# Padding three small SBUF tables so that the big ones start at multiples of 64 bytes

## The chip, the cores and the metric

The kernel runs on one core of a Trainium2 chip. The time is the device time of one execution in microseconds (us), as a median of three runs; lower is better. A profile of one execution on the chip goes with it. All work is in float32, and there is one launch.

## The reference

The input is 256 tokens of 1024 features. A first block computes a root-mean-square norm, one wide projection (queries, keys, values, a recurrent input and three gates), banded attention with 16 heads, a causal convolution with a gated linear recurrence, the two output projections, a merge, a residual, and a gated feed-forward layer. A second block runs four more gated feed-forward layers, a chunked spatial gating unit between the first two of them, and stick-breaking attention between the last two:

```python
def swiglu(h, w_in, w_out):
    gu = h @ w_in
    gate, up = jnp.split(gu, 2, axis=-1)
    return (jax.nn.silu(gate) * up) @ w_out
...
x = x + FFN_RES_SCALE * swiglu(rms_norm(x, ffn_norm[i, 0]), ffn_w_in[i, 0], ffn_w_out[i, 0])
h = rms_norm(x, mix_norm[i])
...
return rms_norm(x, final_norm)
```

Nearly all arithmetic is products of 256 tokens with weight matrices that are read once each.

## The kernel before

**Weights.** The host lays all weights out as 240 groups of 1 MB, 128 partitions by 2048 elements, in the order in which they are used (`PLAN`). SyncE's queue loads a group into one of three buffers `raw` (`load`). A group is two chunks of 128 by 1024. `prep` turns a chunk into two float32r tiles: ScalarE copies `raw` into `h` (line 162), which rounds it, and VectorE writes the remainder `raw - h` into `l` (line 163). There are eight buffers each of `h` and `l`, and `refill` prepares chunks up to seven ahead of their use.

**Activations.** They are split in the same way into a high and a low part: `xh` and `xl` (8 feature tiles of 128 by 256 each), and the four tables `rr0` to `rr3` of that size.

**Products.** A product of two split operands is three TensorE matmuls into the same PSUM bank (`mm3`): high by high, high by low, low by high. All matmuls are issued at line 210. In most of them the stationary operand is 128 columns of `h` or `l`, and the moving one is 256 columns of `xh`, `xl` or an `rr`: a chunk is 24 of these. In the value projection, the spatial gate's first half and the last layer's output (`pe_nat`, `pe_rn`) it is the other way round: 128 columns of the activations are stationary and 512 columns of `h` or `l` move. A few others are plain float32, of which the trace records two matmuls for each one that is issued, and 56 are bfloat16.

**Order.** Everything is issued in one fixed order written by hand. While TensorE works on a chunk, small generators (`rounds`) issue a step of other work each: scaling by the norm's factor, the gates' functions, attention, the recurrence.

**Placement.** `sb(name, shape)` takes a table out of one pool. The tables lie in the order in which they are asked for, each rounded up to 32 bytes per partition, behind a start at a multiple of 64 bytes (byte 16512). `par` is 200 floats, 800 bytes, which is 32 past a multiple of 64. So `x0` to `x3`, `xh`, `xl`, `rr0` to `rr3` and `sa` all start 32 bytes past a multiple of 64. `sa` is 2072 floats, 8288 bytes, again 32 past one, so the next tables (`sb`, `sc`, `sd`, `sf`, `sg`, `sh`, `ident`, `ones`) start at multiples of 64. Behind some small tables follow `ntri`, `nones`, `identb`, `maskb` (at multiples), more small tables, and then `raw`, `h` and `l`, all 32 bytes past one. Slices inside the big tables step by multiples of 64 bytes.

Of the kernel before, what the change touches and what calls it, by code (L numbers as in the profile page):

```python
# [100 lines left out]
NPAR = 0  # L101
# [5 lines left out]
class Builder:  # L107
# [67 lines left out]
        self.gens.append(gen)  # L175

    def refill(self, most=2):
        """prepares the weights to come, more of them once the first loads have landed"""
        ahead = LA if self.ci > 12 else 4
        for _ in range(most):  # L180
            if self.preps < self.ci + ahead:
                self.prep()
# [97 lines left out]
        self.nc.gpsimd.tensor_tensor(dst, src, self.mhalf[:, 0:src.shape[1]], op=ALU.pow)  # L280

    def bcast_mm(self, bank, half, col, start):
        """a factor per token (partition) to a row on every partition"""
        for t in range(2):
            self.mm(bank[:, half, t * 128:(t + 1) * 128], col[:, t:t + 1].to_broadcast([128, 128]), self.ident,
                    start and t == 0, True)

    def stats_a(self, pool=None, kv=False):
        """squares to the per-token factor column"""
        nc = self.nc  # L290
        self.st = (pool or self.acc)()
        self.R, self.rcol = (self.Rkv, self.rckv) if kv else (self.Rt, self.rc)
        self.stat_mm(self.sq[0], self.st, 0, True)
        nc.vector.tensor_scalar(self.v2, self.st[:, 0, 0:2], 1.0 / D, 1e-6, op0=ALU.mult, op1=ALU.add)
        self.rpow(self.rcol, self.v2)

    def stats_b(self):
        """the factors on every partition"""
        self.bcast_mm(self.st, 1, self.rcol, False)
        self.nc.scalar.activation(self.R, self.st[:, 1, :], AF.Copy)  # L300

# [15 lines left out]

    def setup(self):
        nc, dram = self.nc, self.dram
        self.P = self.sb("par", [128, NPAR])  # L320
        self.X = [self.sb(f"x{p}", [128, 2, 256]) for p in range(4)]
        self.XS = (self.sb("xh", [128, 8, 256], F32R), self.sb("xl", [128, 8, 256], F32R))
        self.RR = [self.sb(f"rr{i}", [128, 8, 256], F32R) for i in range(4)]
        self.SA = self.sb("sa", [128, 8 * 259])
        self.SL = {c: self.sb("s" + c, [128, 2048]) for c in "bcdfgh"}
        self.ident = self.sb("ident", [128, 128])
        self.ones = self.sb("ones", [128, 128])
        self.mhalf = self.sb("mhalf", [128, 2])
        self.Rt = self.sb("rt", [128, 256])
        self.R1 = self.sb("r1t", [128, 256])  # L330
        self.Rkv = self.sb("rkv", [128, 256])
        self.rckv = self.sb("rckv", [128, 2])
        self.v2 = self.sb("v2", [128, 2])
        self.rc = self.sb("rc", [128, 2])
        self.tiny = self.sb("tiny", [128, 1])
        self.c8 = self.sb("c8", [128, 8])
        self.nc8 = self.sb("nc8", [128, 8])
        self.half = self.sb("half", [128, 24])
        self.sq = self.view("b", 4)
        nc.scalar.dma_start(self.P, dram["par"])  # L340
        x_load = lambda p: nc.sync.dma_start(self.X[p], dram["x"][:, 2 * p:2 * p + 2, :])
        for f in range(2):
            nc.sync.dma_start(self.X[0][:, f, :], dram["x"][:, f, :])  # L343
        self.warm_up()
        for g in range(2):
            t = self.rawp.tile([128, 2048], F32, tag="raw", name="raw")
            for c in range(2):
                if 2 * g + c:
                    x_load(2 * g + c)
                n = 512 if 2 * g + c == 0 else 1024  # L350
                for o in range(c * 1024, (c + 1) * 1024, n):
                    nc.sync.dma_start(t[:, o:o + n], dram["w"][g, :, o:o + n])  # L352
            self.raw[g] = t
        self.loads = 2
        self.load()
        self.gw = self.SL["h"].rearrange("p (a b) -> p a b", b=128)
        make_identity(nc, self.ident)
        nc.gpsimd.memset(self.ones, 1.0)
        nc.gpsimd.memset(self.mhalf, -0.5)
        nc.gpsimd.memset(self.tiny, 2.0 ** -115)  # L360

    def warm_up(self):
        """keeps the tensor engine busy while the first operands are on their way"""
        nc = self.nc
        nc.vector.memset(self.SL["c"][:, 0:64], 0.0)
        junk = self.SL["c"][:, 0:64].bitcast(BF16)
        bank = self.wk()
        for _ in range(40):
            self.mm(bank[:, 0, 0:128], junk, junk, True, True)
        nc.scalar.preload_act_table_set("exp_and_others")  # L370
# [7 lines left out]
        for gi in range(2):  # L378
            self.group(kinds, lambda c, h, l, s: self.pe_k(h, l, s[2], self.XS, outs), fills=fills[gi])

    # ---------------------------------------------------------------- block 1
    def block1(self):
        nc, dram = self.nc, self.dram
        SA, SL, RR = self.SA, self.SL, self.RR
# [7 lines left out]
        xr = SA.rearrange("p (a b) -> p a b", b=259)  # L392
# [4 lines left out]
        it = SL["d"].rearrange("p (a b) -> p a b", b=256)  # L397
# [1 line left out]
        gb = SL["g"].rearrange("p (a b) -> p a b", b=256)  # L399
        ga = SL["h"].rearrange("p (a b) -> p a b", b=256)  # L400

        # xr
        w = ("A", "w_in")
        b = [self.wk(), self.wk()]
        self.start_k((("K", "w_in"),) * 2, [b[0][:, 0, :], b[0][:, 1, :], b[1][:, 0, :], b[1][:, 1, :]])
# [31 lines left out]
        for p in range(4):  # L437
            a_group(mul_ev(ga, p))

        # v, tokens on partitions  # L440
        V = SL["c"].rearrange("p (t c) -> p t c", c=1024)
        for cg in range(2):
            banks = [self.wk(), self.wk()]
# [7 lines left out]
            for gi in range(2):  # L451
                self.group((("K", "w_in"),) * 2,
                           lambda c, h, l, s: self.pe_nat(h, l, s[2], self.XS, banks),
                           end=(lambda: self.spawn(v_ev())) if gi else None)

        # attention state
        qk = self.carve("b", 0, 2, 512)
        PT = self.carve("b", 1024, 2, 384) + self.carve("d", 1536, 1, 384) + self.carve("f", 1536, 1, 384)
        bias = self.carve("d", 0, 2, 768)
# [82 lines left out]

        qk_group(0)

        # rnn_out
        accs = [self.acc() for _ in range(4)]
        for r in range(4):
            self.group((("R", "rnn_out"),) * 2,
# [10 lines left out]
        for j in range(1, 8):  # L559
            qk_group(j)  # L560

        # attn_out, merged with the recurrent branch
        accs2 = [self.acc() for _ in range(4)]
        MH, ML = RR[0], RR[1]
        for r in range(3):
# [13 lines left out]
        self.tail_group("attn_out", (6, 7), lambda k: (OH[:, k, :], OL[:, k, :]), accs2, merge, merge_l)  # L579
        self.drain()  # L580

        # w_o and the residual
        gf = lambda k: ("norm_ffn_g", k)
        for half in range(2):
            b = [self.wk(), self.wk()]
# [10 lines left out]
            for gi in range(2):  # L596
                self.group((("K", "w_o"),) * 2,
                           lambda c, h, l, s: self.pe_k(h, l, s[2], (MH, ML), outs),
                           end=fin if gi else None)
# [106 lines left out]
                    yield  # L706

    def tail_group(self, name, ks, zf, accs, fin, fin_l):
        """last two rows of weights, output by output, each pair finished as it comes"""
        g = self.gi  # L710
        assert [c[:3] for c in PLAN[g]] == [("R", name, k) for k in ks], (PLAN[g], name, ks)
        hl = [self.take()[:2] for c in range(2)]
        self.rounds(1)
        for p in range(4):
            for o in (2 * p, 2 * p + 1):
                for i, k in enumerate(ks):
                    s = slice(o * 128, o * 128 + 128)
                    zh, zl = zf(k)
                    self.mm3(accs[p][:, o % 2, :], hl[i][0][:, s], hl[i][1][:, s], zh, zl, start=False, stop=(i == 1))
            fin(p)  # L720
            if p:
                fin_l(p - 1)
        fin_l(3)
        self.rounds(1)
        self.refill()

    # ---------------------------------------------------------------- feed-forward
    def ffn(self, n, fin, fin_l, stats=None, nat=False, more=None):
        nc = self.nc
        a, r = ("A", f"{n}_in"), ("R", f"{n}_out")  # L730
# [56 lines left out]
        return accs  # L787

    def pe_rn(self, h, l, zh, zl, accs, first, last, banks=range(4)):
        """a row block of weights as the moving operand: tokens on partitions"""  # L790
        for b in banks:
            t, cg = divmod(b, 2)
            out = accs[b].rearrange("p a b -> p (a b)")
            s, ts = slice(cg * 512, cg * 512 + 512), slice(t * 128, t * 128 + 128)
            self.mm(out, zh[:, ts], h[:, s], first, False)
            self.mm(out, zh[:, ts], l[:, s], False, False)
            self.mm(out, zl[:, ts], h[:, s], False, last)
# [19 lines left out]
            self.split_l(p, self.X, g, xs)  # L817
        return fin, fin_l

    # ---------------------------------------------------------------- block 2  # L820
    def block2(self):
        nc, dram, P = self.nc, self.dram, self.par
        SA, SL, RR = self.SA, self.SL, self.RR

        # end of block 1: x2 = h * r1 * g1, next input x2 * r2 * g2
        XG = self.view("c", 4)

        def fin(p, bank):
# [71 lines left out]
        self.ffn("f3", fin, fin_l, stats=(lambda: self.stats_a(kv=True), sb3))  # L900
        self.squares(self.X, self.sq)

        # keys and values from the state before that feed-forward layer
        Kt = SL["c"][:, 0:512].rearrange("p (a b) -> p a b", b=256)
        Vt = SL["c"][:, 512:1024].rearrange("p (t c) -> p t c", c=256)
        kb, vb = self.acc(), self.acc()
# [33 lines left out]
        assert not self.gens  # L940

    def final_bank(self, b, bank):
        """the last norm and the output"""
        nc = self.nc
        t, cg = divmod(b, 2)
        flat = bank.rearrange("p a b -> p (a b)")
# [1 line left out]
        s0, s1, v, r = self.ss[:, t, 0:1], self.ss[:, t, 1:2], self.v2[:, t:t + 1], self.rc[:, t:t + 1]  # L948
# [15 lines left out]
    def sgu(self, fin, fin_l):  # L964
# [29 lines left out]
                if c % 2:  # L994
                    yield

        # gate half, tokens on partitions
        def v_ev(banks, cg):
            sl = slice(cg * 512, (cg + 1) * 512)
            for t in range(2):  # L1000
# [33 lines left out]
        a = ("A", "a_in")  # L1034
# [8 lines left out]
        UH, UL = (RR[0], RR[1]), (RR[2], RR[3])  # L1043

        def mix(p):
            """token mixing of feature tiles 2p, 2p+1 and the product with u"""
            bank = self.wk()
            for f in range(2):
                c = 2 * p + f
# [203 lines left out]


def stick_order():
    """heads in the order of the tiles: two heads of neighbouring key/value heads each"""
    cols = []
    for T in range(8):
        kp, t = divmod(T, 4)
        for h in (2 * kp * 4 + t, (2 * kp + 1) * 4 + t):  # L1260
            cols.extend(range(h * 64, h * 64 + 64))
    return np.array(cols)
# [82 lines left out]
```

## Time and profile before

| | |
|---|---|
| median of 3 runs | 1462.52 us (1462.49 to 1462.91) |
| span of the profiled execution, first to last instruction | 1460.8 us |
| outside the span (median less span) | 1.7 us |
| TensorE, matmuls | 1451.3 us busy, 99% |
| TensorE, weight loads | 1413.2 us busy, 97% |
| VectorE | 950.9 us busy, 65% |
| ScalarE | 734.7 us busy, 50% |
| weights moved | 257 MB read, 177 GB/s over the span |

The time of an execution is its span and what lies around it; the profiled one is 1.7 us short of the median. Matmuls are pipelined: the profile gives each a duration from its start to its modelled end, and they overlap. What a matmul costs in a stream is therefore not its duration but the distance from its start to the next one's start, called the pitch below.

### The profile page before, as it was taken

What the parts mean: (1) busy time and instruction counts of PE and PEld (TensorE: products, weight loads), DVE (VectorE), ACT (ScalarE), POOL (GpSimd) and SP (SyncE); (2) the same over time, 40 slices, a digit from 0 to 9 for tenths busy, and PEclk for the clock granted to TensorE, in tenths of its full rate; (3) what the DMA queues carried; (4) which work ended last, traced back from release to release, by engine and by line L of the source; (5) the groups of instructions that cost most, each with busy time, mean ns of one, the idle gap of its engine ahead of it and who ended that gap; (6) DMA issues with size and microseconds to landing.
All of it is one profiled execution on the core that took longest, in us unless ns stands there. A gap on an engine that the chain in (4) does not pass through costs nothing.

```text
span 1460.8 us, 26958 instructions
## 1 busy us (share of the span) xinstructions
PE 1451.3 (99%) x11548; PEld 1413.2 (97%) x11548; DVE 950.9 (65%) x1316; ACT 734.7 (50%) x1094; POOL 24.8 (2%) x57
## 2 busy tenths in 40 slices
PE   9999999999999999999999999999999999999998
PEld 9998999999999999998999999999999998999997
DVE  6976677665557765576775655567655576655563
ACT  5677465544445544455445444445444467544442
POOL 0000000000000000000000000000000000000000
PEclk9999999999999999999999999999999999999999
DMA  8555444454454555546444555544555542445451
GB/s 293 199 186 198 177 163 174 173 202 174 176 188 155 194 185 189 195 178 221 170 155 164 189 186 177 191 181 164 190 196 195 179 174 87 159 145 196 180 182 49
DMA packets 37624, 260.31 MB, mean 178 GB/s; under 512 B 4224, under 2 KB 4608, under 8 KB 7040
## 3 DMA queue, kind: packets, MB, share of 16 engines
q1 hardware_dynamic: 36288, 253.77, 48.7%
q0 software_dynamic: 1072, 4.72, 1.0%
q8 instruction: 90, 1.47, 0.4%
q14 instruction: 30, 0.25, 0.0%
q10 hardware_dynamic: 144, 0.10, 0.0%
HBM read 257.53 MB, written 1.05 MB: 177 GB/s over the span
## 4 chain that ended last, share of the span: by engine, by line
PE 99%; DMA 0%; ACT 0%; DVE 0%; SPq 0%; issue 0%; POOLq 0%; POOL 0%
PE wk L210 62%; PE acc L210 36%; DMA raw<-w 0%; PE acc L521 0%; PE wk L521 0%; ACT sf L959 0%; ACT sd L949 0%; DVE l L163 0%; ACT h L162 0%; SPq L352 0%; SPq L343 0%; DVE sf L950 0%; POOLq L1341 0%; POOL rc L280 0%; ACT sh L1134 0%
## 5 line engine op out<-in xcount | busy, mean ns | idle before, releaser
L163 DVE TENSOR_TENSOR l<-raw,h 128x1024 fp32r<-128x1024 f32 (+1 forms) x479 | 570.8, 1219 | 241.0 <-ACT h L162 240.4
L210 PE MATMUL wk<-xh,h 128*128 128x256 f32 x2272 | 646.8, 285 | 1.2 <-ACT h L162 1.2
L210 PE MATMUL wk<-xh,l 128*128 128x256 f32 x2272 | 643.9, 283 | 0.1
L210 PE MATMUL wk<-xl,h 128*128 128x256 f32 x2272 | 643.6, 283 | 0.0
L162 ACT ACTIVATE h<-raw 128x1024 fp32r<-128x1024 f32 (+1 forms) x479 | 485.7, 1044 | 64.6 <-PE acc L210 30.1
L210 PEld LDWEIGHTS wk<-xh,h 128*128 128x128 f32 x2272 | 436.7, 192 | 4.0 <-ACT h L162 1.8
L210 PEld LDWEIGHTS wk<-xl,h 128*128 128x128 f32 x2272 | 436.7, 192 | 0.5
L210 PEld LDWEIGHTS wk<-xh,l 128*128 128x128 f32 x2272 | 436.5, 192 | 0.6 <-DVE l L163 0.6
L210 PE MATMUL acc<-rr,h 128*128 128x256 f32 x2016 | 367.2, 284 | 0.0
L210 PEld LDWEIGHTS acc<-rr,h 128*128 128x128 f32 x2016 | 314.3, 192 | 1.9 <-issue 1.9
L210 PE MATMUL acc<-rr,l 128*128 128x256 f32 x1008 | 285.2, 283 | 0.0
L210 PEld LDWEIGHTS acc<-rr,l 128*128 128x128 f32 x1008 | 193.4, 192 | 0.0
L738 ACT ACTIVATE sa<-sa 128x256 f32<-128x256 f32 x110 | 45.4, 417 | 285.6 <-DVE sa L306 285.4
L309 ACT ACTIVATE rr<-sa 128x256 fp32r<-128x256 f32 (+1 forms) x122 | 52.7, 439 | 185.8 <-DVE sa L743 128.9
L306 DVE TENSOR_TENSOR sa<-wk,rt 128x512 f32<-128x512 f32 x92 | 62.3, 686 | 91.0 <-PE wk L210 73.1
L310 DVE TENSOR_TENSOR rr<-sa,rr 128x256 fp32r<-128x256 f32 (+1 forms) x122 | 54.2, 451 | 53.3 <-ACT rr L309 53.3
L210 PE MATMUL acc<-h,rr 128*128 128x512 f32 (+1 forms) x208 | 63.1, 374 | 0.0
L210 PEld LDWEIGHTS acc<-h,rr 128*128 128x128 f32 x208 | 38.7, 189 | 6.7
L258 ACT ACTIVATE xh<-x,par 128x256 fp32r<-128x256 f32 x56 | 25.2, 501 | 33.8 <-DVE x L316 18.6
L210 PE MATMUL acc<-l,rr 128*128 128x512 f32 (+1 forms) x104 | 38.9, 374 | 0.0
L743 DVE TENSOR_TENSOR sa<-sa 128x256 f32<-128x256 f32 x88 | 37.0, 428 | 0.0
L210 PE MATMUL wk<-rr,h 128*128 128x256 f32 x192 | 34.8, 283 | 0.0
(253 smaller groups left out, 970.2 us busy)
## 6 DMA issues: line engine op xcount, KB each, us to landing
raw<-w SPq DMA_DIRECT2D x237, 1024.0 KB, 4.9
sd<-bias POOLq DMA_DIRECT2D x8, 384.0 KB, 3.3
raw<-w SPq DMA_DIRECT2D x3, 512.0 KB, 8.3
sh<-gates SPq DMA_DIRECT2D x1, 1024.0 KB, 9.1
out<-sf SPq DMA_DIRECT2D x4, 256.0 KB, 2.1
x<-x SPq DMA_DIRECT2D x3, 256.0 KB, 7.4
raw<-w SPq DMA_DIRECT2D x2, 256.0 KB, 4.4
sa<-ws POOLq DMA_DIRECT2D x1, 512.0 KB, 3.7
```

The source lines that it names most:

```text
L162: nc.scalar.activation(h[:, s], raw[:, s], AF.Copy)
L163: nc.vector.tensor_tensor(l[:, s], raw[:, s], h[:, s].bitcast(F32), op=ALU.subtract)
L210: self.nc.tensor.matmul(out, lhsT, rhs, start=start, stop=stop, skip_group_check=True)
L258: self.nc.scalar.activation(xs[0][:, k, :], src[p][:, f, :], AF.Copy, scale=self.par(*g(k)))
L306: self.nc.vector.tensor_tensor(dst, bank, self.Rpair(), op=ALU.mult)
L309: self.nc.scalar.activation(zh, src, AF.Copy)
L310: self.nc.vector.tensor_tensor(zl, src, zh.bitcast(F32), op=ALU.subtract)
L738: nc.scalar.activation(t[:, 0, :], t[:, 0, :], AF.Silu)
L743: nc.vector.tensor_tensor(t[:, 1, :], t[:, 0, :], t[:, 1, :], op=ALU.mult)
```

## The change

Three tables are asked for with more columns than are used, and then cut to the columns used. `par` grows from 800 to 896 bytes, `sa` from 8288 to 8320, and `rckv` (8 bytes, 32 with rounding) to 64. No instruction is added, removed or moved; the order and all shapes are the same. Some comments go too.

```diff
-        self.P = self.sb("par", [128, NPAR])
+        self.P = self.sb("par", [128, 224])[:, 0:NPAR]
...
-        self.SA = self.sb("sa", [128, 8 * 259])
+        self.SA = self.sb("sa", [128, 2080])[:, 0:8 * 259]
...
-        self.rckv = self.sb("rckv", [128, 2])
+        self.rckv = self.sb("rckv", [128, 16])[:, 0:2]
```

By the sizes, `x0` to `x3`, `xh`, `xl`, `rr0` to `rr3` and `sa` move up by 96 bytes, to multiples of 64. The tables behind `sa` move by 128 and keep their place within 64 bytes: `sb` to `sh`, `ident` and `ones` at multiples, `rt`, `r1t` and `rkv` 32 past one. All behind `rckv` moves by 160: `raw`, `h` and `l` come to lie at multiples of 64, and `ntri`, `nones`, `identb` and `maskb` 32 past one.

## Rows read from the trace of the kernel before

**Rows 1.** The page's head and part 1: busy time, share of the span, instructions.

```profile
span 1460.8 us, 26958 instructions
...
PE 1451.3 (99%) x11548; PEld 1413.2 (97%) x11548; DVE 950.9 (65%) x1316; ACT 734.7 (50%) x1094; POOL 24.8 (2%) x57
```

**Rows 2.** The page's part 4: the chain that ended last, by engine.

```profile
PE 99%; DMA 0%; ACT 0%; DVE 0%; SPq 0%; issue 0%; POOLq 0%; POOL 0%
```

**Rows 3.** The page's part 2: granted TensorE clock in 40 slices, in tenths.

```profile
PEclk9999999999999999999999999999999999999999
```

**Rows 4.** Groups of TensorE instructions by shape; out<-moving,stationary, count | busy, mean ns | idle.

```profile
L210 PE MATMUL wk<-xh,h 128*128 128x256 f32 x2272 | 646.8, 285 | 1.2 <-ACT h L162 1.2
...
L210 PE MATMUL acc<-h,rr 128*128 128x512 f32 x176 | 56.1, 390 | 0.0
...
L210 PE MATMUL acc<-sb,sh 128*128 128x256 f32 x32 | 7.6, 379 | 0.0
...
L210 PE MATMUL acc<-ident,x 128*128 128x128 f32 x32 | 3.7, 275 | 0.0
...
L210 PE MATMUL wk<-sa,ones 128*128 128x512 f32 x4 | 1.9, 594 | 0.0
```

**Rows 5.** Timeline of TensorE, 700 to 704 us: start us, length us, what.

```profile
699.83 0.28 PE L210 MATMUL wk<-xl,h 128*128 128x256 f32 x1
...
703.91 0.28 PE L210 MATMUL wk<-xh,l 128*128 128x256 f32 x1
```

**Rows 6.** Timeline of TensorE, 1434 to 1438 us.

```profile
1434.10 0.39 PE L210 MATMUL acc<-l,rr 128*128 128x512 f32 x1
...
1434.78 0.39 PE L210 MATMUL acc<-l,rr 128*128 128x512 f32 x1
```

**Rows 7.** Timeline of TensorE, 8 to 21 us.

```profile
8.01 0.41 PE L210 MATMUL wk<-xl,h 128*128 128x256 f32 x1
...
9.93 0.41 PE L210 MATMUL wk<-xl,h 128*128 128x256 f32 x1
...
10.31 0.28 PE L210 MATMUL wk<-xh,h 128*128 128x256 f32 x1
...
10.67 0.28 PE L210 MATMUL wk<-xh,h 128*128 128x256 f32 x1
```

**Rows 8.** Timeline of TensorE, 46.9 to 49.5 us.

```profile
47.27 1.89 PE L210 MATMUL acc<-sb,sh 128*128 128x256 f32 x8
```

**Rows 9.** Timeline of TensorE, 663.2 to 665.4 us.

```profile
663.71 1.88 PE L210 MATMUL wk<-sa,ones 128*128 128x512 f32 x4
```

**Rows 10.** Timeline of TensorE, 1292 to 1297 us.

```profile
1292.39 3.74 PE L210 MATMUL acc<-ident,x 128*128 128x128 f32 x32
```

**Rows 11.** Timeline of TensorE, 732.2 to 733.8 us.

```profile
732.61 0.39 PE L210 MATMUL wk<-sa,sc 128*128 128x128 f32 x2
...
733.28 0.39 PE L210 MATMUL wk<-sa,sd 128*128 128x128 f32 x2
```

**Rows 12.** Timeline of TensorE, 1203.5 to 1206 us.

```profile
1204.22 0.51 PE L210 MATMUL wk<-rr,ntri 128*128 128x384 f32 x2
1204.57 0.40 PE L210 MATMUL wk<-rr,nones 128*128 128x256 f32 x2
```

**Rows 13.** Timeline of TensorE, 1352 to 1353.2 us.

```profile
1352.38 0.28 PE L210 MATMUL wk<-xh,h 128*128 128x256 f32 x1
1352.49 0.28 PE L210 MATMUL wk<-xl,h 128*128 128x256 f32 x1
1352.61 0.28 PE L210 MATMUL wk<-xh,l 128*128 128x256 f32 x1
```

**Rows 14.** Groups of VectorE instructions by shape.

```profile
L163 DVE TENSOR_TENSOR l<-raw,h 128x1024 fp32r<-128x1024 f32 x477 | 569.4, 1222 | 239.4 <-ACT h L162 238.9
...
L686 DVE SCALAR_TENSOR_TENSOR sd<-sd,sb 128x1024 f32<-128x1024 f32 x2 | 2.4, 1216 | 0.0
```

**Rows 15.** The page's part 6: DMA issues; KB each, median us to landing.

```profile
raw<-w SPq DMA_DIRECT2D x237, 1024.0 KB, 4.9
```

## Prediction

> **What bounds the kernel now.** I read the busy times first: TensorE is busy for 99% of the span, its weight loads for 97%, the next engine for 65% [rows 1]. The chain that ended last is TensorE for 99% [rows 2], and the granted clock is at the upper of its two levels, 2.4 GHz, in every slice [rows 3]. So the time is the sum of the distances between matmul starts. I counted matmuls in the groups by shape and read their pitch in the timeline. 10,368 float32r matmuls move 256 columns (2,272 each for three products into `wk` and the rest into `acc` and from `rr` in the same form) and 552 move 512 [rows 4]. From 699.83 to 703.91 us lie 34 pitches: 120.0 ns each [rows 5]. For 512 columns three pitches take 0.68 us: 226.7 ns [rows 6]. 10,368 x 0.120 = 1244.2 and 552 x 0.2267 = 125.1, together 1369.3 of the 1460.8 us. The other 91.5 us are the start, the tail, attention and other plain float32 matmuls.
>
> At 2.4 GHz, 256 columns take 106.7 ns and 512 take 213.3. Each matmul thus pays 13.3 ns beyond its columns, whatever its length: the time of 32 columns, which is 128 bytes of a partition. The question is whether that excess comes from the operands lying 32 bytes past a multiple of 64.
>
> **The change part by part.** It removes and adds no instruction; only addresses move. What could change is how long an instruction takes to read its operands.
>
> *TensorE, the excess.* Near the start the same matmuls, at the same addresses, go at another pitch: nine pitches from 8.01 to 9.93 us, 213.3 ns each, and then 120 ns from 10.31 us on [rows 7]. 213.3 ns is 256 columns at 1.2 GHz, the lower level, with no excess (the clock row shows tenths for slices of 36 us and does not resolve this stretch). Were the excess 32 cycles of the array, this pitch would be 240 ns; were it 13.3 ns fixed per instruction, 226.7. So it is neither; it appears only when columns are consumed at full rate, as a limit on supplying operands does.
>
> Plain float32 takes two cycles a column and says the same from the other side. With both operands at multiples of 64, eight matmuls of 256 columns take 1.89 us to the end of the last, which lasts 0.379: (1.89 - 0.379) / 7 = 216 ns, 2.5 more than 2 x 106.7 [rows 4, 8]. With the moving operand 32 bytes past (`sa`), 512 columns take (1.88 - 0.594) / 3 = 429 ns, 2 more than 4 x 106.7 [rows 4, 9]. At half the rate neither has an excess worth naming, and the offset does not show.
>
> No float32r matmul of this trace has its moving operand at a multiple of 64, so the price after the change has to be bounded. From above: 120 ns, no change. From below: a stream with no excess, 106.7 ns plus the 2.5 of the plain matmuls, 109 ns; and 213.3 + 2.5 = 216 for 512 columns. [...] Where the columns take only 106.7 ns, 128 columns of float32 weights set the pitch: (3.74 - 0.275) / 31 = 112 ns with weights 32 bytes past (`x`) [rows 4, 10], and six pitches in 0.67 us, 112 ns, with weights at multiples (`sc`, `sd`) [rows 11]. Every 256-column matmul here has such a load. I take 112, the nearest row of a stream that waits for nothing but its weights; 109 stays as the low end.
>
> Which operand matters? With weights at a multiple (`ntri`) but the moving operand 32 past, 384 columns take 175 ns, 15 more than 160 [rows 12]: aligned weights alone give nothing. The moving operand is what the change would have to help, and all of them (`xh`, `xl`, `rr`, `h`, `l`) move to multiples. An extra piece read at the end of an unaligned stream, of fixed size, fits an excess that does not depend on the length; that is why I think alignment more likely than not to be the cause, though half the excess may remain.
>
> First after a 512-column matmul, whose length hides the load, a 256-column one takes 110 to 113 ns, the next 120 [rows 13]. That even an unaligned stream can go at some 113 when the weights are there early is the row for a partial gain.
>
> [...]
>
> *The rest of TensorE.* `ntri`, `nones`, `identb` and `maskb` go the other way, to 32 past. They are the weights of 80 matmuls; at up to 13 ns each that is 1 us. I take nothing, since the offset of weights did not show above.
>
> *VectorE, ScalarE.* VectorE takes 1222 ns for 1024 columns of `raw` and `h` at 32 past, and 1216 for `sd` and `sb` at multiples [rows 14]. I cost the alignment there at nothing; both engines work beside TensorE. Their cover stays: VectorE's 950.9 us over 479 chunks are 1.99 us a chunk, against 24 x 0.112 = 2.69 us of TensorE; it becomes the bound only below 83 ns a matmul.
>
> *DMA.* A group lands in 4.9 us [rows 15]; TensorE would use one in 48 x 0.112 = 5.4, with three buffers. Hidden, if closer than now.
>
> *Sum.* 10,368 x (120 - 112) = 82.9 us, 552 x (226.7 - 216) = 5.9 us: 1460.8 - 88.8 = 1372.0, and with the 1.7 us outside the span **1373.7 us**. With 109 it is 1460.8 - 114.0 - 5.9 + 1.7 = 1342.6; with 114, half the excess, 1460.8 - 62.2 - 3.0 + 1.7 = 1397.
>
> **The rivals.**
>
> *Nothing changes.* The supply at full rate is limited to 256 columns in 120 ns wherever the tables lie. For it: the offset shows in no row at half rate [rows 8 to 11], nor on VectorE. Against it: a plain limit on the rate would grow with the columns, and the excess is 13.3 ns for 256 and for 512. Then 1462.5 us.
> [...]
>
> *A small gain.* Only part of the excess goes, and the pitch falls to between 114 and 119 [rows 13]: at 117, 10,368 x 3 = 31 us, 1431.
>
> *Full streaming speed.* The load hides fully and 109 ns is reached: 1342.6. Against it, 112 in both rows that wait for loads [rows 10, 11].
>
> *Slower.* The stream and the load beside it, now both from the start of a 64-byte piece, meet in the same place at each step. The price is what a load in full overlap adds now, 120 - 113 = 7 ns [rows 13], once more: 127 ns, 10,368 x 7 = 72.6 us, 1535. It decides from 120.3 ns on. Against it: both have the same offset now too, 32, so they already keep step.
>
> **How the numbers follow.** Some 112 ns (110.5 to 114): 0.48. Full streaming speed: 0.10. A small gain: 0.10. Nothing: 0.26. Slower: 0.06. The time is that of the first, 1373.7, whose own range is 1357 to 1397. To leave out no more than 2 in 10, the range has to reach the case of no change on one side and the full speed on the other: 1342 to 1464. A difference of 0.2%, 2.9 us, is about what a measurement of this kernel can tell from none: faster 0.68, same 0.26, slower 0.06.
>
> **What would show it right or wrong.** Right: the timeline shows starts 112 ns apart in stretches of 256 columns, and 216 for 512; the counts and the 91.5 us of other work stay; VectorE's 1222 ns stay and its share rises to some 69%. A pitch of 120 everywhere says that the excess does not come from the offset. A pitch of 112 with a time well above 1374 would mean that TensorE now waits, for `h`, `l` or a load that lands late. 512 columns at 216 with 256 at 120 would put the limit on the weight load, and the gain at 5.9 us.

## The result, and the profile after

The changed kernel takes 1435.55 us (median of four, 1435.30 to 1435.84) against 1462.67 for the kernel before beside it: ratio 0.9816, 95% interval 0.9802 to 0.9830. It is faster, by 27 us where 89 were forecast.

The head, part 1, part 4 and the weight loads of the page of the changed kernel:

```profile
span 1434.0 us, 26959 instructions
...
PE 1423.5 (99%) x11548; PEld 1384.3 (97%) x11548; DVE 949.8 (66%) x1316; ACT 734.9 (51%) x1094; POOL 24.8 (2%) x57
...
PE 98%; DMA 0%; ACT 0%; DVE 0%; SPq 0%; issue 0%; POOLq 0%; POOL 0%
...
raw<-w SPq DMA_DIRECT2D x237, 1024.0 KB, 4.9
```

The bound is the same as in [rows 1, 2]: the count of matmul records, 11,548, stands. TensorE's busy time fell by 27.8 us, from 1451.3 to 1423.5, and the span by 26.8; its idle time went from 9.5 to 10.5 us.

Groups by shape of the changed kernel, TensorE's for [rows 4] and then VectorE's for [rows 14]:

```profile
L210 PE MATMUL wk<-xh,h 128*128 128x256 f32 x2272 | 641.1, 282 | 1.8 <-ACT h L162 1.8
...
L210 PE MATMUL acc<-h,rr 128*128 128x512 f32 x176 | 56.3, 392 | 0.0
```

```profile
L163 DVE TENSOR_TENSOR l<-raw,h 128x1024 fp32r<-128x1024 f32 x477 | 569.7, 1222 | 239.6 <-ACT h L162 239.4
```

The 512-column group didn't get shorter (390 to 392 ns), and VectorE's 1222 ns are what they were.

The timeline of TensorE, for [rows 5]: 33 pitches from the first line to the second.

```profile
700.14 0.28 PE L210 MATMUL wk<-xh,l 128*128 128x256 f32 x1
...
704.03 0.28 PE L210 MATMUL wk<-xh,l 128*128 128x256 f32 x1
```

3.89 us / 33 = 117.9 ns where the kernel before had 120.0. The same instructions in another stretch of the same kernel, 39 pitches:

```profile
48.76 0.28 PE L210 MATMUL wk<-xh,l 128*128 128x256 f32 x1
...
53.18 0.28 PE L210 MATMUL wk<-xh,l 128*128 128x256 f32 x1
```

4.42 / 39 = 113.3 ns. So there are two levels, and the forecast's 112 is nearly met, but only here and there: of 10,314 steps from a 256-column float32r matmul to the next matmul, where that has 256 columns too, 8,733 have 117 to 119 ns and 1,419 have 113 or 114. A stretch, that is a row of such matmuls with no other between them, keeps one level from end to end, up to 1,500 matmuls; only after an interruption by other matmuls is the level another.

512 columns, for [rows 6] (nine pitches), and the beginning, for [rows 7] (nine pitches):

```profile
1405.89 0.39 PE L210 MATMUL acc<-l,rr 128*128 128x512 f32 x1
...
1407.95 0.39 PE L210 MATMUL acc<-l,rr 128*128 128x512 f32 x1
```

```profile
8.16 0.41 PE L210 MATMUL wk<-xh,l 128*128 128x256 f32 x1
...
10.08 0.41 PE L210 MATMUL wk<-xh,l 128*128 128x256 f32 x1
```

2.06 / 9 = 229 ns, slower than the 226.7 of before; and still 213.3 ns at the beginning, where the granted clock of this trace is 0.50 (7.6 to 10.9 us). The trace before reads 1.00 at the place of [rows 7], at the same pitch, so the prediction had the level from the pitch alone. No trace gives the clock in GHz: the prediction's two levels stand for 1.00 and 0.50, and 106.7 ns for 256 columns and 213.3 for 512 at 1.00 are estimates from the 213.3 ns that 256 columns take at 0.50. Over all steps of the trace, interruptions included, the 256-column mean went from 120.85 to 118.14 ns and the 512-column mean from 228.5 to 230.8: 10,314 x 2.71 = 28.0 us gained and 538 x 2.3 = 1.2 us lost make the 26.8.

### The profile page after: what moved, and what is told of

Read it like the earlier page. It is cut to its first block, busy times and chain, and to the rows that moved or that the text cites. A ratio compares the mean times of both kernels' runs of the same rounds, so it can differ in the third digit from the quotient of the medians.

```text
span 1434.0 us, 26959 instructions
## 1 busy us (share of the span) xinstructions
PE 1423.5 (99%) x11548; PEld 1384.3 (97%) x11548; DVE 949.8 (66%) x1316; ACT 734.9 (51%) x1094; POOL 24.8 (2%) x57
## 3 DMA queue, kind: packets, MB, share of 16 engines
q1 hardware_dynamic: 36288, 253.77, 49.5%
## 4 chain that ended last, share of the span: by engine, by line
PE 98%; DMA 0%; ACT 0%; DVE 0%; SPq 0%; issue 0%; POOLq 0%; POOL 0%
PE wk L210 62%; PE acc L210 36%; DMA raw<-w 0%; PE acc L521 0%; PE wk L521 0%; ACT sf L959 0%; ACT sd L949 0%; DVE l L163 0%; ACT h L162 0%; SPq L352 0%; SPq L343 0%; DVE sf L950 0%; POOLq L1341 0%; POOL rc L280 0%; ACT sh L1134 0%
## 5 line engine op out<-in xcount | busy, mean ns | idle before, releaser
L210 PEld LDWEIGHTS wk<-xh,h 128*128 128x128 f32 x2272 | 427.4, 188 | 4.5 <-issue 2.0
L210 PEld LDWEIGHTS wk<-xh,l 128*128 128x128 f32 x2272 | 429.8, 189 | 0.9 <-DVE l L163 0.9
L210 PE MATMUL acc<-rr,h 128*128 128x256 f32 x2016 | 359.8, 281 | 0.0
L210 PEld LDWEIGHTS acc<-rr,h 128*128 128x128 f32 x2016 | 309.9, 189 | 1.9 <-issue 1.9
L210 PEld LDWEIGHTS acc<-rr,l 128*128 128x128 f32 x1008 | 189.9, 188 | 0.0
```

What stands on the lines that cost most here:

```text
L210: self.nc.tensor.matmul(out, lhsT, rhs, start=start, stop=stop, skip_group_check=True)
```

## The experiments

**Theory and rivals.** The theory on record: an unaligned moving stream reads a piece more, and multiples of 64 take it away. The rivals after the result: the weights' alignment does it; or neither operand's own address counts, only how the two lie to each other, because a weight load runs beside every moving stream (loads busy for 97% of the span, matmuls for 99%, [rows 1]). "Distance" below is the weights' address less that of the activations, as 256-column matmuls use them, modulo 256 bytes. Before the change it is 0 by the order and sizes of the tables (the activations at byte 25504 of a partition, the weights at 163232, 538 x 256 apart). The padding of `par` moves both; that of `sa` and `rckv` lies between them, 32 bytes each, and makes it 64.

**1. A table by offset**, without the rest of the kernel: stretches of 48 matmuls in the kernel's order, moving operand and weights each 0, 32, 64 or 96 bytes past a multiple of 128.

```
for mo in (0, 8, 16, 24):            # float32 elements
    for wo in (0, 8, 16, 24):
        for n, k in ...:             # xh, xl moving, h, l weights
            mm(out[:, n, :], h[:, wo+128*k : wo+128*k+128], xh[:, mo+256*k : mo+256*k+256])
            ...
```

> Streams of float32r matmuls alone, with no loads, no VectorE and no ScalarE work beside them: 16 pairs of byte offsets (moving operand at 0, 32, 64, 96; weights at 0, 32, 64, 96), each 4 x 48 matmuls of 256 columns, and 2 x 24 of 512 columns with the roles exchanged; between the stretches a few plain float32 matmuls. The kernel computes nothing of the reference: it copies its input to the output. If the two offsets alone set the pitch: 120 ns at 32 and 32, and 113 to 118 at 0 and 0, as in the traces of before and after. If the weights' offset sets it, the table has the same pitch along the moving offset, if the moving operand's, along the weights'. If other engines or the loads of weights set it: one pitch in all 16 pairs. If there are two levels at 0 and 0 that the interruption chooses, as the trace of after suggests (113.3 and 117.7 ns), the four stretches of that pair differ.

Pitches from the starts in the trace, without the first steps of a stretch (the median of a place's four stretches, of two for 512 columns):

```
256 columns        weights +0   +32    +64    +96     512 columns   +0     +32    +64    +96
moving +0             120.0   118.3  117.8  117.4                 227.1  233.4  233.4  234.3
moving +32            116.7   120.0  118.3  117.8                 233.4  227.0  233.4  233.4
moving +64            117.8   116.7  120.0  118.3                 229.1  233.3  226.6  233.3
moving +96            120.0   117.8  117.2  120.0                 233.4  228.9  233.4  227.4
```

Two stretches from the timeline, both with the moving operand at +0: weights at +0 (tile `mawa`, 42 pitches, 5.03 us), then at +64 (`mawc`, 36 pitches, 4.24 us).

```profile
43.84 0.28 PE L41 MATMUL mawa<-xh,l 128*128 128x256 f32 x1
...
48.87 0.28 PE L41 MATMUL mawa<-xh,l 128*128 128x256 f32 x1
...
95.95 0.28 PE L41 MATMUL mawc<-xh,l 128*128 128x256 f32 x1
...
100.19 0.28 PE L41 MATMUL mawc<-xh,l 128*128 128x256 f32 x1
```

The diagonal is the same four times: with both at a multiple of 64 it is 120.0 ns, the highest value of the table (one unequal pair, +96 and +0, has it too). Alignment gives nothing; how the two lie to each other is what counts. The theory on record falls here, and so does the expectation of 113 to 118 at +0 and +0, which took that pair for the changed kernel's: its distance is 64. The two places at distance 64 ran at 117.8 in all their stretches. For 512 columns equal offsets are best.

**2. One half of the padding in the kernel.** First without the padding of `rckv` (activations at multiples of 64, weights 32 past one), then that padding alone (activations 32 past, weights at multiples). Distance 32 in both.

```
 # 1: from the changed kernel
-self.rckv = self.sb("rckv", [128, 16])[:, 0:2]
+self.rckv = self.sb("rckv", [128, 2])
 # 2: from the kernel before
-self.rckv = self.sb("rckv", [128, 2])
+self.rckv = self.sb("rckv", [128, 16])[:, 0:2]
```

> The change without the padding of rckv: activations at multiples of 64, weights (raw, h, l) 32 bytes past one. If the moving operand's offset makes the gain: about 1435.5 us, pitch 113 to 118. If the weights' offset makes it: 1462.5 us, pitch 120. If both are needed, or only that they agree: 1462.5 or slower.

> The padding of rckv alone: weights (raw, h, l) at multiples of 64, activations 32 bytes past one. If the moving operand's offset makes the gain: 1462.5 us, pitch 120. If the weights' offset makes it: about 1435.5 us. If both are needed, or only that they agree: 1462.5 or slower.

1448.68 us (ratio 0.9906, 0.9891 to 0.9921) and 1448.86 us (0.9912, 0.9895 to 0.9928), with mean pitches of 119.22 and 119.20 ns for 256 columns and 234.4 and 234.3 for 512. Neither of the times expected, 1435.5 and 1462.5 us, came. It doesn't matter which of the two is aligned: equal distances, equal times.

**3. Distance 128**, both at multiples of 64:

```
-self.rckv = self.sb("rckv", [128, 16])[:, 0:2]
+self.rckv = self.sb("rckv", [128, 32])[:, 0:2]
```

> The change with rckv padded to 128 bytes: weights at multiples of 128 as the activations already are, instead of 64 past one. If only the offset within 64 bytes counts: 1435.5 us and the same two levels of pitch. If it is that within 128: the level of 113.3 ns everywhere, some 9,000 x 4.4 ns = 40 us less, 1396 us.

1454.76 us (0.9945, 0.9931 to 0.9960), mean pitch 119.75: activations and weights are at multiples of 64 as in the changed kernel, and it is 19 us slower. Neither 1435.5 nor 1396 us, the two expected, came, so the offset within 64 or within 128 bytes alone does not decide.

**4. A table by distance**, with the stretches of the first one and only the weights moved, in steps of 32 bytes to 992 and at a few places between.

> Streams alone as in the first table, now by the distance between the two operands: the moving operand stays where it is, the weights are shifted by 0 to 992 bytes in steps of 32 (32 rows), and by 4, 8, 16, 48, 80 and 112 bytes; 3 x 48 matmuls of 256 columns each, and 16 distances for 512 columns. The kernel computes nothing of the reference. If only the distance within 128 bytes counts: the same four pitches (120, 118.3, 117.8, 117.4 ns) return every 128 bytes. If higher bits of it count, as the kernel with the weights at multiples of 128 suggests (1454.8 us, not 1462.5): a table that repeats every 256, 512 or 1024 bytes, with rows below 116.7 ns in it. If a distance exists at which the two reads do not meet: a row at 113.3 ns, or at 109 if those 113.3 still hold some of it.

```
bytes   0      4      8      16     32     48     64     80           96
ns      120.0  118.4  115.6  118.3  118.3  117.7  117.8  118.7-120.0  117.4-120.0
bytes   112    128          160    192    224
ns      120.0  118.6-120.0  120.0  117.8  116.7-117.8
```

The values at multiples of 32 return every 256 bytes, four times over. The table's best multiple of 32 is 224; 8 bytes are better still. No row reached 113.3 or 109, and 8 bytes were not tried in the kernel.

**5. Both at multiples of 64, distance 0 again, and distance 224.**

```
-self.rckv = self.sb("rckv", [128, 16])[:, 0:2]
+self.rckv = self.sb("rckv", [128, 64])[:, 0:2]     # distance 0
+self.rckv = self.sb("rckv", [128, 56])[:, 0:2]     # distance 224
```

> The changed kernel with 192 bytes more in front of the weights: all activations and weights still lie at multiples of 64 bytes, but the weights' addresses now differ from those of the activations by a multiple of 256, as they did before the change. Theory (only the distance between moving operand and weights, modulo 256 bytes, matters): the pitch of the 256-column matmuls is back at 120.0 in every stage and that of the 512-column ones at 226.7, the time at that of the kernel before, 1462 +/- 2 us. Rival (multiples of 64 bytes help in themselves, as the change says): about 1436 us, as the changed kernel.

> The changed kernel with 160 bytes more in front of the weights (weights at 32 bytes past a multiple of 64, activations at a multiple): distance 224 modulo 256, which had the lowest pitch of the multiples of 32 in the table by distance, 116.7 against 117.8 ns at distance 64. Theory (distance alone, the table holds in the kernel): 10,300 matmuls x (120.0 - 116.7) = 34 us off the kernel before, less some 3.5 us for the 512-column ones (233.4 against 226.7), so 1430 us, 1425 to 1437. Rival (multiples of 64 help): 1449 to 1462 us, since the weights lie 32 bytes past a multiple of 64. A third possibility: the stages in which distance 64 ran at 113.3 have no counterpart at 224, and then it is 1434 to 1442.

Distance 0: 1462.60 us, ratio 1.0001 (0.9991 to 1.0010). The timeline, 33 pitches in 3.96 us, 120.0 ns:

```profile
700.21 0.28 PE L210 MATMUL wk<-xh,l 128*128 128x256 f32 x1
...
704.17 0.28 PE L210 MATMUL wk<-xh,l 128*128 128x256 f32 x1
```

That is the whole change as it is described, all activations and weights at multiples of 64, and it gains nothing. Distance 224: 1436.34 us (0.9819, 0.9804 to 0.9833), not the 1430 of the table. Its 256-column mean is 118.02 ns, as good as the changed kernel's 118.14, and its 512-column mean 234.3 against 230.8, worth 538 x 3.5 = 1.9 us. The time is in the range of the third possibility on record, but for another reason than the one given there: distance 224 has two levels in the kernel as well, 116.7 ns for some 5,800 matmuls (the stretch from 471 us on) and 117.8 for some 3,800 (the stretch from 282 us on). Distance 128 of experiment 3 has 118.7 and 120.0.

**6. Short weights and fine distances**, in streams alone:

```
-ws = slice(wo + 128*k, wo + 128*k + 128)
+ws = slice(wo + 128*k, wo + 128*k + w)       # w = 32, 64, 96, 128
```

> Streams of float32r matmuls alone (the output is not the reference's, x is copied to it). Weights of 32, 64, 96 and 128 columns at distances 0, 8 and 64: if the pitch over the stream is time in which the weight load and the moving stream meet, then it grows with the columns of the weights at distance 0 (a third of a step per 32 columns from a floor of 113.3 up to 120.0) and is the same 113.3 at short weights whatever the distance. If it is a fixed cost of a matmul, it is 120.0 at distance 0 for all four widths. Distances of 8 to 252 bytes in steps of 4: expected lowest at 8 (115.6 in the table by distance) or beside it. Moving operand and weights both moved by 16 bytes at distance 8: again 115.6. Ten interruptions by plain matmuls at distances 8, 64 and 224: if the level is chosen at an interruption, 64 shows 117.7 after some and 113.3 after others; if it is a matter of what else the core does, 117.7 after all of them. 512 columns at 8, 24, 64, 224 and 248: 229 to 234.

```
weights of       32 columns     64           96           128 columns
distance 0       113.3, 117.8   113.3-113.4  115.9-116.1  120.0
distance 8       113.3, 117.6   116.7        116.7        115.6
distance 64      113.3, 116.7   119.0-119.1  117.1        113.3, 117.8
```

At distance 0 the pitch falls with the weights' columns from 120.0 over 116 to 113.3 at 64 columns, as it should if the load beside the stream costs the time, though not by equal thirds; but of the two stretches with 32 columns one ran at 117.8. At 8 and 64 it isn't in order at all. Against the expectation, short weights are not at 113.3 whatever the distance. The width of the weights takes part, but how isn't told by this table. Of the finer distances 8 bytes stay the best; the others (12 to 72 and 216 to 252) lie between 116.7 and 121.9. One value contradicts "the distance alone": both operands moved by 16 bytes more, at the same distance of 8, give 120.0 instead of 115.6. There the place itself counts too. Ten interruptions left distance 8 at 115.6 and distance 224 at 116.7 every time, while distance 64 went between 113.3 and 117.8. So both levels of the changed kernel come without anything that its other engines do.

**7. A plain matmul ahead of the stretches.** 24 plain float32 matmuls, of one column, then of 128, each put ahead of the stretch that follows a broadcast of the norm's factors (`bcast_mm`), a row block of 512-column matmuls (`pe_rn`) or a token mixing of the spatial gate.

```
 def mm3(self, out, wh, wl, xh, xl, start, stop):
+    while start and self.kick:
+        self.kick -= 1
+        self.mm(out[:, 0:1], self.ones, self.ident[:, 0:1], True, True)   # then 0:128
     self.mm(out, wh, xh, start, False)
 ...
 # at the end of bcast_mm, pe_rn and a token mixing
+    self.kick = 1
```

> The changed kernel with one plain float32 matmul of one column (ones by one column of ident, into a bank that the next matmul starts anew) put ahead of the stretch of 256-column float32r matmuls that follows a broadcast of factors, a 512-column row block or a token mixing (some 30 in all, about 0.2 us each, so up to 6 us spent). Nothing else is changed. Theory: at distance 64 there are two patterns in which the load and the stream go on side by side, 117.7 and 113.3 ns, and the entry after an interruption decides which; in the table of streams an odd number of plain one-column matmuls was followed by 113.3 and an even number by 117.8. So most of the 118 stretches that follow the broadcasts (about 6,000 matmuls) and the row blocks (about 800) turn to 113.3: up to 6,800 x 4.4 = 30 us less, 5 us spent, 1405 to 1420 us. Rival: the level belongs to the stage (what DVE, ACT and the DMAs do in SBUF beside it) and not to the entry: the stretches stay at 117.7 and the time is 1437 to 1442 us.

> The same with a plain matmul of 128 columns in place of the one of one column. In the table of streams one such matmul, and two, were followed by 113.3 and three by 117.8; in the changed kernel four, six or eight instructions of the broadcasts were followed by 117.7 nearly everywhere. Theory (the entry decides): other stretches than with one column turn to 113.3, anything from 1405 to 1440 us, and the level of each stretch again holds from its entry to its end. Rival (the stage decides): every stretch as in the changed kernel, 1438 to 1444 us.

1412.99 us (0.9661, 0.9645 to 0.9678) and 1412.74 us (0.9658, 0.9644 to 0.9673): 22.6 us below the changed kernel for 24 matmuls more, and in the ranges expected of the entry (1405 to 1420 us for one column); the rival, that the stage sets the level, expected 1437 us or more. The timeline of the first, before and behind one such matmul (a plain float32 matmul has two records): 18 pitches in 2.12 us, 117.8 ns, then 21 pitches in 2.38 us, 113.3 ns.

```profile
281.01 0.28 PE L211 MATMUL wk<-xh,l 128*128 128x256 f32 x1
...
283.13 0.28 PE L211 MATMUL wk<-xh,l 128*128 128x256 f32 x1
283.25 0.28 PE L211 MATMUL wk<-ident,ones 128*128 128x1 f32 x2
283.40 0.36 PE L211 MATMUL wk<-xh,h 128*128 128x256 f32 x1
...
284.41 0.28 PE L211 MATMUL wk<-xh,l 128*128 128x256 f32 x1
...
286.79 0.28 PE L211 MATMUL wk<-xh,l 128*128 128x256 f32 x1
```

The steps of 117 to 119 ns fall from 8,733 to 2,310. Against the expectation, the width made no difference: the same stretches turned. Behind the 512-column row blocks every second stretch of 96 turned only: five of nine stood at 117.8.

**8. More of them, and the control without the padding.** Inside the mixings (no longer behind them) and the column sums of the squares, behind the gates, and none behind the row blocks (29 in all); and the 24 of the last experiment in the kernel before.

```
 def pe_rn(...):
-    self.kick = 1
 def stat_mm(...):
+    self.mm(st[:, 0, 8:9], self.ones, self.ident[:, 0:1], first, True)   # it starts the bank now
 ...
 def mix(p):
+    self.mm(bank[:, 0, 0:1], self.ones, self.ident[:, 0:1], True, True)
 ...
-    self.kick = 1        # behind a mixing
 # behind the gates of a pair
+    self.kick = 1
```

> The changed kernel again, with the plain one-column matmul in more places (inside the token mixings and the column sums, behind the gates) and none after the 512-column row blocks, where the two kernels with kicks had every second stretch of 96 at 117.7. Some 2,300 of the 256-column matmuls still ran at 117 to 119 there. Theory (the entry decides, an odd number of plain matmuls in it leads to 113.3): of these about 1,700 turn (48 to 456 behind the gates, 360 behind the last mixings, 240 behind the column sums, 430 beside the row blocks), 1,700 x 4.4 = 7.5 us less, about 2 us less spent on kicks after row blocks and 4 us more on the new ones: 1404 to 1411 us. Rival (the odd number was chance): some of the stretches that ran at 113.3 fall back, 1413 to 1430.

> The kernel before (distance 0) with the kicks of the first kernel with kicks. In the tables by offset and by distance every stretch at distance 0 ran at 120.0 whatever stood ahead of it. Theory (the second pattern exists only where the operands lie 64 bytes apart): no stretch changes, the some 30 kicks cost 3 to 6 us, 1464 to 1469 us. Rival (the kick works by itself and the padding isn't needed): 1413 to 1440 us.

With more: 1406.71 us (0.9619, 0.9603 to 0.9635), as expected, and the fastest of all versions here. The page's head and part 1, and 36 pitches in 4.08 us of its timeline, 113.3 ns:

```profile
span 1404.9 us, 27069 instructions
...
PE 1395.4 (99%) x11606; PEld 1356.2 (97%) x11606; DVE 949.0 (68%) x1316; ACT 734.6 (52%) x1094; POOL 25.8 (2%) x57
```

```profile
900.07 0.28 PE L211 MATMUL wk<-xh,l 128*128 128x256 f32 x1
...
904.15 0.28 PE L211 MATMUL wk<-xh,l 128*128 128x256 f32 x1
```

793 steps of 117 to 119 ns are left. All nine stretches behind row blocks now run at 113.3 without a plain matmul of their own: the stretch ahead of the first row block did, and the level came through the blocks, as 117.8 did in the changed kernel.

Without the padding: 1467.92 us (1.0038, 1.0023 to 1.0053). Its timeline, 12 pitches in 1.44 us behind the plain matmul:

```profile
290.41 0.28 PE L211 MATMUL wk<-ident,ones 128*128 128x1 f32 x2
...
291.23 0.28 PE L211 MATMUL wk<-xh,l 128*128 128x256 f32 x1
...
292.67 0.28 PE L211 MATMUL wk<-xh,l 128*128 128x256 f32 x1
```

120.0 ns, and 5.35 us / 24 = 0.22 us spent on each. At distance 0 no second level came.

**9. Which interruption leads to which level**, at distance 64, in streams alone.

```
for cols in (1, 128, 64, 256):
    for count in (1, 1, 1, 2, 2, 2, 3, 3, 3, 4, 4, 5, 5, 6, 6, 7, 8):
        for t in range(count):
            mm(sep[:, t % 2, 0:cols], ones, ident[:, 0:cols])
        stream("...", 16)        # 48 matmuls
```

> Streams of float32r matmuls alone at distance 64 (the output is not the reference's, x is copied to it), 48 to a stretch, with 1 to 8 plain float32 matmuls of 1, 128, 64 or 256 columns between them, each number up to three times in a row; then between stretches of 512-column float32r matmuls in various numbers, stretches of other lengths, pauses without any matmul, and distances 0, 8 and 224. If an odd number sets the level: 113.3 after each odd number and 117.8 after each even one, whatever came before. If each plain matmul turns the level over: it alternates after 1, 1, 1, stays after 2, 2, 2. If the time of the entry decides (the rest of a step between the last plain matmul and the first of the stretch): the level depends on the columns of the interruption as well, is the same for the same interruption wherever it stands, and a pause gives now one, now the other. Distance 0: 120.0 throughout, distance 8 115.6, distance 224 116.7.

Two stretches behind the same single one-column matmul, 45 pitches in 5.30 us, then 39 in 4.42:

```profile
16.19 0.28 PE L41 MATMUL sep<-ident,ones 128*128 128x1 f32 x2
...
16.64 0.28 PE L41 MATMUL one<-xh,l 128*128 128x256 f32 x1
...
21.94 0.28 PE L41 MATMUL one<-xh,l 128*128 128x256 f32 x1
22.06 0.28 PE L41 MATMUL sep<-ident,ones 128*128 128x1 f32 x2
...
23.10 0.28 PE L41 MATMUL one<-xl,h 128*128 128x256 f32 x1
...
27.52 0.28 PE L41 MATMUL one<-xl,h 128*128 128x256 f32 x1
```

117.8 and 113.3 ns: the same interruption gives both levels. With 1, 64 or 128 columns, an odd number turned the level over in all 27 cases (117.8, 113.3, 117.8 after one, one, one). An even number led to 117.8 each time with 1 and 64 columns, and kept the level each time with 128. With 256 columns no such rule holds. None of the three expected rules covers all of it: the entry decides, together with what the stretch ahead left behind. Of the other interruptions in this run, blocks of one, three and six 512-column matmuls changed the level in some cases, those of 12 and 24 followed a stretch at 117.8 and kept it, and after eight pauses of 2.2 us without a matmul seven stretches ran at 113.3 and one at 117.8. Nor does "an odd number turns over" hold throughout in the kernel: with an odd number in each column sum and mixing, stretches at 113.3 were followed by 113.3.

## Why the prediction was wrong

- **Bound, counts, cover: right.** TensorE alone sets the time (98% of the chain that ended last); VectorE's 1222 ns and the 4.9 us of a weight group stayed; VectorE's share is 66%, and 68% in the fastest version. `ntri` and the rest, now 32 bytes past, cost nothing that the time shows: a 384-column matmul takes some 177 ns (mean of 32) where it took 175.
- **The step that failed: "An extra piece read at the end of an unaligned stream, of fixed size, fits an excess that does not depend on the length".** Aligned streams at distance 0 pay the whole 13.3 ns (120.0 ns, experiments 1 and 5). That the excess is equal for the two lengths seems to be chance: the lowest pitches that any long stretch reached are 113.3 for 256 columns and 226.6 for 512, 17/16 of the estimates of 106.7 and 213.3 at a granted clock of 1.00, which is for these two lengths a part in proportion to the length, and no address took it away. For 512 columns at distance 0 that is all of the 13.3; for 256 it is 6.7. The other 6.7 went at distance 0 with weights of 64 columns, and at distance 64 in the lower pattern, which points to the weight load beside the stream; how it comes about isn't shown. Only those went in any run: an estimate of 10,368 x 6.7 = 69 us at most, of which the change got 28.
- **"Aligned weights alone give nothing. The moving operand is what the change would have to help": wrong.** With only the weights at multiples of 64 it was 13.5 us faster, with only the activations 13.6 (experiment 2). The row for 384 columns was no evidence: there, too, a load ran beside the stream (188 ns).
- **The dismissal of the rival that was nearest.** "Slower" came nearest to what the runs show, in that it let stream and load meet at each step, and was put aside with "both have the same offset now too, 32, so they already keep step". That sentence describes the kernel before as the bad case; read on, it says that parting them gains. The rows of a first matmul behind a 512-column one, at 110 to 113 ns [rows 13], gave what the author took for the price of that meeting, 120 - 113 = 7 ns, and it was added once more to the 120 of before; that it could be taken off them was used for a partial gain alone.
- **The 112 ns** from rows taken to wait for weight loads were near the level that exists, 113.3, but not near the one that 85% of the steps took, 117.8. So the term of 82.9 us in the sum measured 28.0. No run shows that the load sets the 112 of those rows. That one distance has two patterns was not foreseen.
- **512 columns: wrong in sign.** 216 was forecast, a gain of 5.9 us; distance 0 was their best, and they lost 1.2 us.
- The time lies in the range, near the 1431 us of the case called a small gain, which had a chance of 0.10. That is luck: the case supposed that alignment takes a part of the excess, and by experiment 5 it takes none.

What is shown: the pitch goes with the distance of the two operands, in the kernel at five distances, all multiples of 32 (256-column means of 120.85 ns at 0, 119.22 at 32, 118.14 at 64, 119.75 at 128, 118.02 at 224), and in streams, where the values at multiples of 32 return every 256 bytes; and it does not go with the alignment of either to 64 (120.0 ns with both at multiples, experiment 5). That the two meet in reading the memory is argued from this and from the weights of 64 and 96 columns at distance 0 (113.3 to 113.4 and 115.9 to 116.1 ns against 120.0), and not shown.

## What to carry to other kernels

Where weight loads run beside float32r streams, look at the distance between the two operands' tables and not at the alignment of each; one small tile padded by a few sizes tells in as many runs which is best, and the longest stage (here 256 columns) decides. Measure the pitch stretch by stretch: where one shape has two levels that hold from entry to end, a matmul of one column ahead of the stretch may turn it, and gave back some 4 us net for each us spent on it here. An excess that two lengths share may be two different costs; a third shape, or the same one without its neighbour, tells.

## What was not expected of the hardware

- The pitch of 256-column float32r matmuls returns with the distance every 256 bytes, and ranges from 113.3 to 121.9 ns. Equal places (120.0) are among the worst for 256 columns and the best for 512 (226.6 to 227.4, against 228.6 to 234.3 elsewhere).
- At distance 64 two patterns, 113.3 and 117.8 ns, last for over a thousand matmuls and, in the kernel, through row blocks of 512-column ones. Distances 128 and 224 have two as well, closer together (118.7 and 120.0, 116.7 and 117.8); with weights of 128 columns, distances 0 and 8 had one each (120.0 and 115.6), whatever stood ahead.
- Plain one-column matmuls at 0.22 us each took 23 us off the changed kernel where there were 24 of them, and 29 where there were 29. What in the entry sets the pattern stays open, and so does the 1/16 by which the 113.3 ns are above half of the 213.3 that 256 columns take at a granted clock of 0.50.
